# The down projection of a decoder layer in seven half-size products: another order of its streams, a fourth raw buffer, and additions moved to DMA

## The chip, the core and the metric

One core of a Trainium2 chip runs the whole layer as one program. Its engines are TensorE (PE, the matrix multiplications), VectorE (DVE), ScalarE (ACT), GpSimd (POOL) and SyncE (SP). Each works through its own instructions in a fixed order and waits on semaphores for the others. Transfers between HBM and on-chip memory are issued here from SP and from POOL, and 16 DMA engines carry them out. The metric is the device time of one execution in microseconds (us). Lower is better.

## The reference

One layer for 512 tokens of width 2048 in f32. The last part of it, the feed-forward block, is what the change is about:

```python
D_MODEL = 2048; SEQ = 512; D_FF = 5632; CONV_W = 3
...
def conv_ffn(h, w_up, w_conv, b_conv, w_down):
    u = h @ w_up                                  # (512, 2048) @ (2048, 11264)
    up = jnp.pad(u, ((0, 0), (CONV_W - 1, 0), (0, 0)))
    conv = b_conv
    for j in range(CONV_W):
        conv = conv + w_conv[j] * up[:, j:j + S]
    gate, val = jnp.split(conv, 2, axis=-1)
    return (jax.nn.silu(gate) * val) @ w_down     # (512, 5632) @ (5632, 2048)
...
        h = rms_norm(x, g_ffn[l]) * (1.0 + sc_f) + sh_f
        x = x + gt_f * conv_ffn(h, w_up[l], w_conv[l], b_conv[l], w_down[l])
```

Ahead of it stand the modulation by `c @ w_ada`, one combined input projection, two attention branches and an output projection. The change leaves these as they are.

## The kernel before

Every product is done in three matrix multiplications: an operand is split into a high part `hi` (rounded to fp32r by ACT, line 127) and a rest `lo` (subtracted by DVE, line 128), and `mm3` (lines 130 to 133) adds hi·hi, hi·lo and lo·hi in a PSUM bank. In the up and the down projection the kernel saves one product in eight: it cuts both operands into 2 by 2 blocks and forms the four result blocks out of seven products of sums and differences of blocks (`r11`, `r21`, `r22`, `t1` to `t4` for the activations). Sums of the weights are formed on the chip, by DVE, from blocks that are loaded raw.

On-chip memory is handed out by hand. There are 76 slots of 128 x 512 f32 (`get`, `put`, a queue that hands out the slot that was freed longest ago), one area `wraw` for raw weights and one area `wsp` for their hi and lo parts. Whoever takes a slot waits for the slot's last users.

**The up projection** (`seven`, line 926) runs pairs of output blocks, seven steps of 24 matrix multiplications with 256 columns each. At the end of a pair `ffn_out` does the convolution and the gating, and `f_out` (line 1341) writes the result and its sums to HBM (`set_d`), seven kinds of 11 tiles each.

**The down projection** (lines 1425 to 1663) reads them back. It is a loop over 110 steps: five phases (`phases`, line 1573) of NK = 22 steps. A phase keeps 4 or 6 accumulators in PSUM banks, and a step adds one block of 128 rows of `w_down` to all of them:

- C for `fp` = 0 and 1 (half of the output columns each): three products (r11, t1, t4), 6 accumulators, 18 matrix multiplications of 128 x 512 a step. `fetch_c` loads 768 KB of weights a step, `form_c` (line 1449) adds two blocks.
- S for `fp` = 0 and 1: three products (t2, t3, r22), 18 matrix multiplications a step. `fetch_s` loads 768 KB into the raw buffer and 256 KB into a slot `x`; `form_s` (lines 1460 to 1463) does three additions and gives `x` back.
- D: the product r21 for both halves, 4 accumulators, 12 matrix multiplications a step, 512 KB of weights and no sums.

The order is C0, C1, S0, S1, D. Step q is made ready like this: `fetch(q + 3)` issues its loads from SP into one of three raw buffers `dr` (512 x 3 columns of `wraw`), `form(q + 2)` does the sums and the split into one of three pairs `dh`, `dl`. The activations are loaded by `load_set` (line 1431) through POOL into a slot and split: r11, t1, t4 four steps ahead in C0; t2, t3, r22 in C1, each when an old pair is dropped (`sets_after`); r21 in D. The first loads of the down projection are written behind the end of `seven`.

At the end of a phase the last two steps are done accumulator by accumulator, and each accumulator is evicted as it is finished (lines 1654 to 1657). In C, `ev_c` adds the products, multiplies by the gate row, adds the residual `x1` (loaded by POOL, line 1485, multiplied in line 1486, added in line 1487) and writes four partial results per token block to HBM (`q1l`, `q1r`, `q2l`, `q2r`, line 1488). In S and D, `ev_s` and `ev_d` load a partial result (`part`, line 1519), multiply the new product by the gate row, add (`leave`, line 1523) and write `out` from SP (line 1524). `gate_row` (lines 786, 787) makes a gate row of two transfers by POOL: a plain load, and a load of a row of `b_ada` that is broadcast and added to the tile by the DMA itself (`accum_op`).

The program is written in this order, but the instruction order on each engine is set by a planner that runs a timeline of its own over the program when it is built: an instruction can be placed behind later ones of the source if the plan does not have its inputs yet. On the chip the order on each engine is then fixed.

Of the kernel before, what the change touches and what calls it, by code (L numbers as in the profile page):

```python
# [18 lines left out]
P = 128  # L19
# [12 lines left out]
def trunk_layer_kernel(  # L32
# [5 lines left out]
    n_slots=76,  # L38
# [22 lines left out]
    cur = [None] * n_slots  # L61
    free = deque(range(n_slots))
    held = {}

    def get(dt=F32):
        i = free.popleft()
        if cur[i] is None or cur[i].dtype != dt:
# [13 lines left out]
    def put(*ts):  # L81
        for t in ts:
            i = held.pop(id(t))
            if isinstance(i, int):
                free.append(i)
            else:
                rfree.append(t)
# [5 lines left out]
    wraw = pool.tile([P, NR * WB], F32, name="wraw")  # L93
# [4 lines left out]
    rfree.extend(wsp[:, o:o + T] for o in range(2 * NH * WB, 2 * NP * DW - T + 1, T))  # L98
    cnt = {"wt": 0, "half": 0, "at": 0}
# [826 lines left out]
    def seven(src, n_pairs, rs, pairs_of_banks, fin, tick=None, near_end=None):  # L926
# [109 lines left out]
        for q in range(len(steps) + AHEAD):  # L1036
# [18 lines left out]
            if near_end and q - AHEAD == len(steps) - 7:  # L1055
                near_end()
# [27 lines left out]
    def reload_mq():  # L1084
        for t in h[:KH]:
            put(*t)
        mqT.extend(reload(mq_d))
# [330 lines left out]


    seven(w_ups, len(UP_PAIRS), operands(h2, tsum), [(bank[2 * i], bank[2 * i + 1]) for i in range(4)], ffn_out)  # L1420
    for t in h2 + [x for ts in tsum for x in ts]:
        put(*t)


    rfree.clear()
    dr = [wraw[:, i * DW:(i + 1) * DW] for i in range(3)]
    dh = [wsp[:, i * DW:(i + 1) * DW] for i in range(NP)]
    dl = [wsp[:, (NP + i) * DW:(NP + i + 1) * DW] for i in range(NP)]
# [29 lines left out]
    def form_s(t, x):  # L1458
        a, d, b = t[:, 0:512], t[:, 512:1024], t[:, 1024:1536]
        V.tensor_tensor(a, a, x, ALU.subtract)  # L1460
        put(x)
# [3 lines left out]
    def fetch_d(_, k, t):  # L1465
# [4 lines left out]
              for n in ("q1l", "q1r", "q2l", "q2r") for fp in range(2) for tt in range(2)}  # L1470

    def gate_of(db):
        t = get()
# [3 lines left out]
    keep = {}  # L1477

    def ev_c(fp):
        g = {}  # L1480

        def base(n, t, tt, src):
            f, r = int(n[1]) - 1, n[2] == "r"
            xt = get()
            G.dma_start(xt, x1_d[fp * 2 + f][2 * r + tt])
            V.tensor_tensor(t, src, g[f], ALU.mult)
            V.tensor_tensor(t, t, xt, ALU.add)
            G.dma_start(part_d[n, fp, tt], t)
            put(xt)

        def ev(i, tt, b):
            t = get()
            if i == 0:
                if tt == 0:
                    g.update({0: gate_of(fp * 2), 1: gate_of(fp * 2 + 1)})
                p = get()
                A.activation(p, b, AF.Copy)
                keep[fp, tt] = p
                base("q1l", t, tt, p)
                put(t)  # L1500
                return
            p = keep[fp, tt]
            V.tensor_tensor(t, b, p, ALU.add)
            if i == 1:
                q = get()
                base("q2r", q, tt, t)
                put(q)
                base("q1r", t, tt, t)
            else:
                base("q2l", t, tt, t)  # L1510
                put(keep.pop((fp, tt)))
                if tt == 1:
                    put(*g.values())
            put(t)
        return ev

    def part(n, fp, tt):
        t = get()
        G.dma_start(t, part_d[n, fp, tt])
        return t  # L1520

# [191 lines left out]
```

## Time and profile before

| | us |
|---|---|
| median of 3 runs | 2752.41 (2751.76 to 2757.78) |
| the profiled execution | 2749.67 |
| its span, first to last instruction | 2747.9 |
| PE busy in the span | 2614.8 (95%) |
| DVE busy | 2171.5 (79%) |
| ACT busy | 1203.0 (44%) |
| POOL busy | 316.4 (12%) |

The profiled execution is 1.8 us longer than its span and 2.7 us shorter than the median. Busy shares are means over stages with different limits; matrix multiplications are pipelined, so that two of them overlap in the records, and the rate is better read from how many of them a stretch holds. The views used below are: the busy time of each engine in chosen stretches (with the number of instructions, the granted share of TensorE's clock, the busy share of the DMA engines and the rate in GB/s), the waits (engine and line, what it waited for, us in total, times, longest), the chain of work that ended last (start, us, what), and the groups of instructions (count, busy us, mean ns of one, idle time before).

### The profile page before, as it was taken

The numbers are of one execution on the slowest core, as the hardware profiler recorded it, in microseconds if no ns is written. First come the engines' busy times: TensorE is split into PE (matmuls) and PEld (weight loads), VectorE is DVE, ScalarE is ACT, GpSimd is POOL, SyncE is SP. The second block draws the span as 40 slices with busy tenths as digits, with TensorE's granted clock in tenths as the row PEclk, the third lists the DMA queues.
The fourth block names the chain that finished last, engine by engine and source line by source line (L and its number), as shares of the span: only waits on it lengthen the run. The fifth ranks groups of instructions, "written<-read, shape, count | busy, mean of one in ns | idle before, by whom it ended". The sixth has DMA issues, their size and how long they took to land. (4 is left out here: it accounts for less than half of the span.)

```text
span 2747.9 us, 40904 instructions
## 1 busy us (share of the span) xinstructions
PE 2614.8 (95%) x15352; PEld 2261.5 (82%) x15352; DVE 2171.5 (79%) x3378; ACT 1203.0 (44%) x1726; POOL 316.4 (12%) x602
## 2 busy tenths in 40 slices
PE   6999999999999999999999999999999979968798
PEld 5887787779987767788789999999999968746576
DVE  7977967698877658872878989899999976877775
ACT  4333434334444464222645555555555553522233
POOL 1001011110032222110000000000000120210110
PEclk8999899999999999999999999999999989989999
DMA  9943137655575578963233343434334476976875
GB/s 351 350 132 97 34 109 222 212 187 192 196 230 163 182 255 292 325 222 116 90 113 132 112 142 122 141 125 134 126 121 134 143 268 203 328 261 204 267 253 172
DMA packets 233099, 512.28 MB, mean 186 GB/s; under 512 B 24858, under 2 KB 66228, under 8 KB 232900
## 3 DMA queue, kind: packets, MB, share of 16 engines
q1 hardware_dynamic: 191508, 394.74, 44.1%
q0 software_dynamic: 41360, 114.92, 12.3%
q8 instruction: 120, 1.97, 0.3%
q14 instruction: 79, 0.65, 0.1%
q10 hardware_dynamic: 32, 0.01, 0.0%
HBM read 452.69 MB, written 56.89 MB: 185 GB/s over the span
## 5 line engine op out<-in xcount | busy, mean ns | idle before, releaser
L127 ACT ACTIVATE wsp<-wraw 128x1024 fp32r<-128x1024 f32 (+1 forms) x446 | 509.9, 1146 | 721.2 <-PE bank L1050 329.2
L1050 PE MATMUL bank<-slot,wsp 128*128 128x256 f32 x2592 | 730.4, 282 | 0.4 <-DVE slot L128 0.4
L1049 PE MATMUL bank<-slot,wsp 128*128 128x256 f32 x2544 | 714.5, 281 | 6.8 <-ACT slot L127 3.5
L1051 PE MATMUL bank<-slot,wsp 128*128 128x256 f32 x2544 | 715.3, 281 | 3.3 <-DVE wsp L128 3.3
L128 DVE TENSOR_TENSOR wsp<-wraw,wsp 128x1024 fp32r<-128x1024 f32 (+1 forms) x446 | 591.3, 1327 | 124.1 <-ACT wsp L127 123.4
L133 PE MATMUL bank<-wsp,slot 128*128 128x512 f32 (+2 forms) x1300 | 509.4, 394 | 12.0 <-DVE slot L128 12.0
L132 PE MATMUL bank<-wsp,slot 128*128 128x512 f32 (+2 forms) x1258 | 498.2, 396 | 19.8 <-DVE wsp L128 19.3
L1050 PEld LDWEIGHTS bank<-slot,wsp 128*128 128x128 f32 x2592 | 488.4, 188 | 0.7 <-DVE slot L128 0.6
L131 PE MATMUL bank<-wsp,slot 128*128 128x512 f32 (+2 forms) x1258 | 445.6, 398 | 45.6 <-ACT wsp L127 35.6
L1049 PEld LDWEIGHTS bank<-slot,wsp 128*128 128x128 f32 x2544 | 480.9, 189 | 8.8 <-ACT slot L127 4.0
L1051 PEld LDWEIGHTS bank<-slot,wsp 128*128 128x128 f32 x2544 | 479.8, 189 | 3.8 <-DVE wsp L128 3.7
L119 ACT ACTIVATE wsp<-wraw 128x1024 fp32r<-128x1024 f32 (+4 forms) x182 | 187.2, 1031 | 359.2 <-PE bank L133 199.9
L120 DVE TENSOR_TENSOR wsp<-wraw,wsp 128x1024 fp32r<-128x1024 f32 (+4 forms) x182 | 215.8, 1187 | 161.7 <-ACT wsp L119 161.4
L131 PEld LDWEIGHTS bank<-wsp,slot 128*128 128x128 f32 x1258 | 239.9, 191 | 104.0 <-ACT wsp L127 39.1
L132 PEld LDWEIGHTS bank<-wsp,slot 128*128 128x128 f32 x1258 | 239.5, 190 | 82.5 <-DVE wsp L128 29.7
L133 PEld LDWEIGHTS bank<-wsp,slot 128*128 128x128 f32 x1300 | 246.8, 190 | 67.3 <-DVE slot L128 13.3
L942 DVE TENSOR_TENSOR wraw<-wraw 128x1024 f32<-128x1024 f32 x192 | 234.0, 1219 | 1.5
L132 PE MATMUL bank<-slot,wsp 128*128 128x512 f32 (+1 forms) x574 | 230.6, 402 | 0.0
L133 PE MATMUL bank<-slot,wsp 128*128 128x512 f32 (+1 forms) x533 | 210.8, 404 | 6.1 <-DVE wsp L120 6.1
L131 PE MATMUL bank<-slot,wsp 128*128 128x512 f32 (+1 forms) x533 | 212.5, 405 | 0.0
L736 DVE SCALAR_TENSOR_TENSOR slot<-slot,c_act,slot 128x512 f32<-128x512 f32 x203 | 149.8, 748 | 40.2 <-DMA slot<-in_w_ada 38.5
L127 ACT ACTIVATE slot<-slot 128x512 fp32r<-128x512 f32 x136 | 82.3, 624 | 108.3 <-DMA slot<-t 23.8
(344 smaller groups left out, 3309.2 us busy)
## 6 DMA issues: line engine op xcount, KB each, us to landing
slot<-in_w_ada SPq DMA_DIRECT2D x344, 256.0 KB, 5.4
wraw<-in_w_ups SPq DMA_DIRECT2D x160, 512.0 KB, 4.5
wraw<-in_w_down SPq DMA_DIRECT2D x110, 512.0 KB, 5.1
wraw<-in_w_in SPq DMA_DIRECT2D x50, 512.0 KB, 3.6
wraw<-in_w_down SPq DMA_DIRECT2D x88, 256.0 KB, 5.3
wraw<-in_w_gs SPq DMA_DIRECT2D x32, 512.0 KB, 4.1
wraw<-in_w_o SPq DMA_DIRECT2D x32, 512.0 KB, 5.0
t<-slot POOLq DMA_DIRECT2D x44, 256.0 KB, 5.3
```

The costliest lines, as they stand in the source:

```text
L119: A.activation(hi, raw[:, :w], AF.Copy)
L120: V.tensor_tensor(lo, raw[:, :w], r32(hi), ALU.subtract)
L127: A.activation(dst_hi, src, AF.Copy)
L128: V.tensor_tensor(dst_lo, src, r32(dst_hi), ALU.subtract)
L131: PE.matmul(o, lh, rh, start=first, stop=False)
L132: PE.matmul(o, lh, rl, start=False, stop=False)
L133: PE.matmul(o, ll, rh, start=False, stop=last)
L736: V.scalar_tensor_tensor(acc, ts[i], c_act[:, k:k + 1], acc, op0=ALU.mult, op1=ALU.add)
L942: V.tensor_tensor(o[:, :WN], a[:, :WN], b[:, :WN], op)
L1049: PE.matmul(o, wh[:, ks], rh, start=first and k == 0, stop=False, skip_group_check=True)
L1050: PE.matmul(o, wh[:, ks], rl, start=False, stop=False, skip_group_check=True)
L1051: PE.matmul(o, wl[:, ks], rh, start=False, stop=last, skip_group_check=True)
```

## The change

In the down projection: D comes third (C0, C1, D, S0, S1). There are four raw buffers and a prefetch distance of four steps. The step's raw `x` and the raw activations come from a ring of three slots of their own, evictions from a second ring (`spare`, five slots), and raw activations are loaded by SP. The eviction of C only copies or adds and writes the products `s1`, `s3`, `s4` to HBM; eight jobs a phase, one after each of the following steps, load a product back, multiply it by the gate row, add `x1` by an accumulating DMA and write the partial result. For S0 and D, the partial result is likewise added by an accumulating DMA, and the result is then written to `out`; S1, now the last phase, loads its partial results eight steps ahead and adds them with DVE and POOL. In the last seven steps of the up projection (`near_down`) the first two sets of activations are loaded and split, step 0 is loaded into slots and split, and the loads of steps 1 to 3 are issued. The slots become 74, with one more inside `wraw` that is retired before the down projection.

```diff
-    n_slots=76,
+    n_slots=74,
...
-    wraw = pool.tile([P, NR * WB], F32, name="wraw")
+    wraw = pool.tile([P, 4 * DW], F32, name="wraw")
...
+    cur[n_slots] = wraw[:, NR * WB:NR * WB + T]
+    free.append(n_slots)
...
-            if near_end and q - AHEAD == len(steps) - 7:
-                near_end()
+            if near_end and q - AHEAD >= len(steps) - 7:
+                near_end(q - AHEAD - len(steps) + 7)
...
-    dr = [wraw[:, i * DW:(i + 1) * DW] for i in range(3)]
+    dr = [wraw[:, i * DW:(i + 1) * DW] for i in (1, 2, 3, 0)]
...
+    def rget():
+        return ring.popleft() if ring else get()
...
+    def eget():
+        return spare.popleft()
...
     def load_set(n, i):
-        raw, hi, lo = get(), getr(), getr()
-        G.dma_start(raw, set_d[n][i])
+        raw = rget()
+        SP.dma_start(raw, set_d[n][i])
+        hi, lo = getr(), getr()
         split(hi, lo, raw)
-        put(raw)
+        rput(raw)
...
     def fetch_s(fp, k, t):
+        SP.dma_start(t[:, 512:1536], rows_of(1, k, fp * 1024, 1024))
         SP.dma_start(t[:, 0:512], rows_of(0, k, fp * 1024 + 512, 512))
-        SP.dma_start(t[:, 512:1536], rows_of(1, k, fp * 1024, 1024))
-        x = get()
+        x = rget()
...
+    def store(n, fp, tt, t):
+        G.dma_start(part_d[n, fp, tt], t)
+        spare.append(t)
...
     def ev_c(fp):
...
         def ev(i, tt, b):
+            t = eget()
             if i == 0:
+                ps[tt] = t
+                A.activation(t, b, AF.Copy)
+                G.dma_start(part_d["s1", fp, tt], t)
                 return
+            V.tensor_tensor(t, b, ps[tt], ALU.add)
+            if i == 2:
+                spare.append(ps.pop(tt))
+            store(("s3", "s4")[i - 1], fp, tt, t)
+            if i == 2 and tt == 1:
+                jobs()
+
+        def base(n, src, tt, f, t):
+            V.tensor_tensor(t, t, g[f], ALU.mult)
+            G.dma_start(t, x1_d[fp * 2 + f][2 * (n[2] == "r") + tt], accum_op=ALU.add)
+            store(n, fp, tt, t)
+
+        def jobs():
+            work = [("q2l", "s4", 0, 1), ("q2r", "s3", 0, 1), ("q2l", "s4", 1, 1), ("q2r", "s3", 1, 1),
+                    ("q1l", "s1", 0, 0), ("q1r", "s3", 0, 0), ("q1l", "s1", 1, 0), ("q1r", "s3", 1, 0)]
...
+            def load(u):
+                if u == 0 or u == 4:
+                    g[1 - u // 4] = gate_of(fp * 2 + 1 - u // 4)
+                ts[u] = eget()
+                G.dma_start(ts[u], part_d[work[u][1], fp, work[u][2]])
...
+            later.extend((None, lambda: load(0)))
+            for u in range(8):
+                later.append((lambda u: lambda: (load(u + 1) if u < 7 and u != 3 else None, go(u),
+                                                 load(4) if u == 3 else None))(u))
...
-    def leave(t, q, db, tb):
-        V.tensor_tensor(q, q, t, ALU.add)
-        SP.dma_start(out[tb * P:(tb + 1) * P, db * 512:(db + 1) * 512], q)
-        put(q)
+    def result(t, n, fp, tt, back):
+        db, tb = fp * 2 + int(n[1]) - 1, 2 * (n[2] == "r") + tt
+        G.dma_start(t, part_d[n, fp, tt], accum_op=ALU.add)
+        SP.dma_start(out[tb * P:(tb + 1) * P, db * 512:(db + 1) * 512], t)
+        back(t)
...
+    def ev_f(fp):
...
+            eng.tensor_tensor(q, q, t, ALU.add)
+            SP.dma_start(out[tb * P:(tb + 1) * P, db * 512:(db + 1) * 512], q)
...
+            if i == 1:
+                V.tensor_tensor(t, t, fin[1], ALU.mult)
+                go("q2r", tt, t, V)
+                go("q2l", tt, t, G)
...
     phases = [(fetch_c, form_c, DW, 0, C_, ev_c(0)), (fetch_c, form_c, DW, 1, C_, ev_c(1)),
-              (fetch_s, form_s, DW, 0, S_, ev_s(0)), (fetch_s, form_s, DW, 1, S_, ev_s(1)),
-              (fetch_d, None, 1024, 0, D_, ev_d(0))]
+              (fetch_d, None, 1024, 0, D_, ev_d(0)),
+              (fetch_s, form_s, DW, 0, S_, ev_s(0)), (fetch_s, form_s, DW, 1, S_, ev_f(1))]
...
         if p == 1:
-            for n in ("r11", "t1", "t4"):
+            for n, m in (("r11", "r21"), ("t1", "t2"), ("t4", "t3")):
                 drop_set(n, i)
-            for n in ("t2", "t3", "r22"):
-                load_set(n, i)
+                load_set(m, i)
+        elif p == 2:
+            drop_set("r21", i)
+            load_set("r22", i)
...
+    def near_down(i):
+        if i == 0:
...
+            for n in ("r11", "t1", "t4"):
+                load_set(n, 0)
+            first_form(first_fetch())
...
+        elif i == 2:
...
+            for n in ("r11", "t1", "t4"):
+                load_set(n, 1)
+        elif i == 4:
...
+            for q in (1, 2, 3):
+                fetch(q)
...
-            fetch(q + 3)
+            fetch(q + 4)
...
+            if q == 0:
+                put(*step0)
+                ring.extend(get() for _ in range(3))
+                spare.extend(get() for _ in range(n_slots - 3 - 3 * NK))
...
+        if later and k < NK - 2:
+            f = later.popleft()
+            if f:
+                f()
```

More of the change, by code (lines that the diff above doesn't have):

```diff
@@ L1469, in trunk_layer_kernel @@
     part_d = {(n, fp, tt): dram.tile([P, T], F32, name=f"{n}_{fp}_{tt}")
-              for n in ("q1l", "q1r", "q2l", "q2r") for fp in range(2) for tt in range(2)}
+              for n in ("q1l", "q1r", "q2l", "q2r", "s1", "s3", "s4") for fp in range(2) for tt in range(2)}
+    later = deque()
     def gate_of(db):
-        t = get()
+        t = eget()
         gate_row(t, 20 + db)
         return t
-    keep = {}
+    def store(n, fp, tt, t):
+        G.dma_start(part_d[n, fp, tt], t)
+        spare.append(t)
@@ L1479, in ev_c @@
     def ev_c(fp):
[L1480 to L1489, printed above, removed]
+        ps, g = {}, {}
         def ev(i, tt, b):
-            t = get()
+            t = eget()
             if i == 0:
[L1494 to L1500, printed above, removed]
-                return
[L1502 to L1506, printed above, removed]
-                put(q)
[L1508 to L1514, printed above, removed]
@@ new lines, in gates, with two_right, one_right @@
+        def gates():
+            for f in range(2):
+                g[f] = get()
+                gate_row(g[f], 20 + fp * 2 + f)
+        def two_right(tt):
+            m, n = us[tt], get()
+            V.tensor_tensor(m, m, g[1], ALU.mult)
+            A.activation(n, m, AF.Copy)
+            result(m, "q2r", fp, tt, spare.append)
+            result(n, "q2l", fp, tt, put)
+        def one_right(tt):
+            V.tensor_tensor(ps[tt], ps[tt], g[0], ALU.mult)
+            result(ps[tt], "q1r", fp, tt, spare.append)
@@ new lines, in jobs, with fin_load @@
+        def jobs():
+            later.extend((None, None, gates, None))
+            for tt in range(2):
+                later.append(lambda tt=tt: two_right(tt))
+                later.append(lambda tt=tt: one_right(tt))
+            later.append(lambda: put(*g.values()))
+        return ev
+    fin = {}
+    def fin_load(fp):
+        for f in range(2):
+            fin[f] = get()
+            gate_row(fin[f], 20 + fp * 2 + f)
+        for tt in range(2):
+            for n in ("q2r", "q2l", "q1r"):
+                fin[n, tt] = get()
+                G.dma_start(fin[n, tt], part_d[n, fp, tt])
@@ L1562, in ev_d, with gate, go @@
     def ev_d(_):
+        ts, g = {}, {}
         def ev(fp, tt, b):
-            t = get()
-            V.tensor_tensor(t, b, base[fp], ALU.mult)
-            leave(t, base[fp, tt], fp * 2, tt)
-            put(t)
+            ts[fp, tt] = eget()
+            A.activation(ts[fp, tt], b, AF.Copy)
+            if (fp, tt) == (1, 1):
+                jobs()
+        def gate(fp):
+            g[fp] = gate_of(fp * 2)
+        def go(fp, tt):
+            t = ts[fp, tt]
+            V.tensor_tensor(t, t, g[fp], ALU.mult)
+            result(t, "q1l", fp, tt, spare.append)
+            if tt == 1:
+                spare.append(g.pop(fp))
@@ L1568, in ev_d, with jobs @@
+        def jobs():
+            for fp in range(2):
+                later.extend((lambda fp=fp: gate(fp), None))
+                later.append(lambda fp=fp: go(fp, 0))
+                later.append(lambda fp=fp: go(fp, 1))
         return ev
```

168 lines of the change are left out of this document (97 added, 71 removed).

## The prediction

> **What bounds the kernel now.** First the page's header and slices, to see which engine carries the time.
>
> ```profile
> span 2747.9 us, 40904 instructions
> PE   6999999999999999999999999999999979968798
> ```
>
> PE is full nearly everywhere; the holes are in the last eight slices, the down projection. So I next ask for the busy time by stage, cut where the phases change (columns: stretch, its length, busy us of PE with the number of matrix multiplications, PEld, DVE, ACT, POOL, granted clock, DMA share, GB/s).
>
> ```profile
> 2110.00:2210.00 100.00, 100.00 (x845) 99.80 (x843) 91.49 (x112) 57.13 (x81) 16.66 (x31) 1.00 0.48 160
> 2211.00:2326.00 115.00, 98.90 (x393) 78.06 (x394) 75.78 (x81) 47.26 (x49) 13.69 (x24) 0.93 0.67 227
> 2327.00:2421.00 94.00, 91.85 (x394) 73.80 (x393) 79.22 (x92) 49.03 (x53) 26.99 (x49) 1.00 0.92 316
> 2421.00:2556.00 135.00, 100.28 (x399) 77.06 (x398) 96.28 (x112) 36.47 (x30) 13.72 (x24) 0.89 0.70 222
> 2556.00:2677.00 121.00, 99.19 (x400) 75.75 (x399) 92.65 (x109) 39.66 (x36) 18.67 (x32) 0.94 0.79 265
> 2677.00:2740.00 63.00, 61.92 (x264) 48.98 (x262) 33.74 (x36) 21.23 (x21) 0.00 (x0) 1.00 0.56 180
> ```
>
> The first row is the end of the up projection, the others are C0, C1, S0, S1, D. D runs without a hole: 61.92 us for 264, or 0.2345 us each. At that rate the stages would take 92.2, 92.4, 93.6, 93.8 and 61.9 us. They lose 22.8 (C0), 1.6 (C1), 41.4 (S0), 27.2 (S1) and 1.1 us (D), 94 in all. This is the whole stock that the change can win, since it leaves every matrix multiplication in place.
>
> Next, what PE waited for: around the start, around C1 to S0, inside S0, and around S0 to S1.
>
> ```profile
> PE bank L133 <- DVE slot L128: 12.0, 3, 6.3
> ...
> PE bank L131 <- ACT wsp L127: 17.6, 1, 17.6
> PE bank L131 <- DVE slot L1503: 7.9, 1, 7.9
> ...
> PE bank L132 <- DVE wsp L128: 8.9, 7, 4.6
> ...
> PE bank L131 <- ACT wsp L127: 15.1, 2, 8.3
> ```
>
> The reader is to see that PE never waits for a transfer itself. At the start it waits for the split of the activations (a slot); at the phase changes for the split of the first weights (`wsp`) and, at C1 to S0, for an eviction that frees a bank (line 1503); inside S0 for the rest of the weights. Behind those the chain of work shows the reason (start, us, what), first inside S0, then at S0 to S1:
>
> ```profile
> 2497.81 1.68 DVE wsp L128
> 2499.51 3.91 DMA wraw<-in_w_down
> 2503.43 0.69 DVE wraw L1460
> ...
> 2508.82 7.84 DMA wraw<-in_w_down
> ...
> 2567.90 6.24 DMA out<-slot
> 2574.21 6.35 DMA slot<-in_w_down
> 2580.57 6.81 DMA slot<-in_w_down
> ```
>
> Inside S0 a load starts when a split has freed its raw buffer, and the next sums wait for it: three buffers do not cover a landing. At S0 to S1 the slot for `x` waits for an `out` store, then one `x` load waits for the one before: the slots are short, not the DMA.
>
> **The change part by part.**
>
> *Start in C0.* Sets 0 and 1, step 0 and the loads of steps 1 to 3 move ahead of the last up matrix multiplication. Groups of the down projection (count | busy us, mean ns | idle before):
>
> ```profile
> L128 DVE TENSOR_TENSOR wsp<-wraw,wsp 128x1536 fp32r<-128x1536 f32 x88 | 154.1, 1754 | 24.0 <-ACT wsp L127 23.7
> L128 DVE TENSOR_TENSOR slot<-slot,slot 128x512 fp32r<-128x512 f32 x66 | 43.7, 686 | 3.5 <-ACT slot L127 3.3
> L1460 DVE TENSOR_TENSOR wraw<-wraw,slot 128x512 f32<-128x512 f32 x44 | 30.4, 690 | 38.1 <-DMA wraw<-in_w_down 25.3 <-issue 6.8 <-DMA slot<-in_w_down 5.9
> L1486 DVE TENSOR_TENSOR slot<-slot,slot 128x512 f32<-128x512 f32 x16 | 10.9, 687 | 1.6 <-DMA slot<-in_b_ada 0.8 <-ACT slot L1497 0.7
> L1487 DVE TENSOR_TENSOR slot<-slot,slot 128x512 f32<-128x512 f32 x16 | 10.8, 685 | 0.4 <-DMA slot<-x 0.4
> L1523 DVE TENSOR_TENSOR slot<-slot,slot 128x512 f32<-128x512 f32 x16 | 10.4, 686 | 1.4 <-DMA slot<-q2l 0.7 <-DMA slot<-q1r 0.6
> L127 ACT ACTIVATE wsp<-wraw 128x1536 fp32r<-128x1536 f32 x88 | 130.3, 1489 | 230.6 <-DVE wraw L1463 129.7 <-PE bank L133 43.7 <-DVE wraw L1449 27.0
> ```
>
> The moved DVE work is ten instructions of 0.69 us (six sets, three splits, one sum), 6.9 us. In the up projection's end DVE is busy 91.49 of 100 us, so over 20 us it has 1.7 us free: the rest displaces splits of the old order, which stood there too. PE then has step 0, 18 x 0.2345 = 4.2 us, while the convolution's end (about six DVE instructions, some 4 us) and the sums and splits of steps 1 and 2 (2.4 us each) want DVE, 8.8 us against 8.4 for two steps. I leave 5 of the 22.8 us; bounds 1 and 16 (only the 6.9 us of moved work gained).
>
> *Phase ends.* In C, an eviction drops from 2 x 6 multiplications and additions with their `x1` loads to four additions and two copies; the multiplications follow one a step. The 16 `x1` additions (10.8 us), and 10 of the 16 in line 1523 (6.5 us), leave DVE, two more go to POOL. The slot waits at C1 to S0 and S0 to S1 go with the rings: `x` no longer queues behind a store. What is late next is DVE: at S0 to S1 two steps of sums and splits (2 x 3.8 us) plus four additions (2.7 us) make 10.3 us in 8.4, so 2 us are lost, and twice that with an imperfect order. I leave 1 us at C0 to C1, 3 at D to S0, 4 at S0 to S1; bounds 0 to 2, 1 to 12, 1 to 17 (the present waits).
>
> *Fourth raw buffer.* It gives each load one more step, 4.2 us, more than the 3.9 us that the chain shows as a wait; of the one wait of 7.84 us it covers 4.2. DVE in S does 3 x 0.69 + 1.75 = 3.8 us a step of 4.2, and holds. I leave 2 us in S0 (bounds 1, 10) and 4 in S1, where eight late loads of partial results and gates arrive in one burst (bounds 1, 9).
>
> *More DMA.* New are 12 stores of products and 16 loads back, 256 KB each, 7.3 MB; accumulating `x1` loads replace plain ones. C1 then moves weights 16.2, sets 8.7, stores 1.6, two gate rows 1.0 and jobs 24 x 0.262 = 6.3, together 33.8 MB; D moves 25.4 MB. What the DMA can move beside this load pattern:
>
> ```profile
> 2345.00:2400.00 55.00, 55.00 (x237) 44.35 (x237) 48.15 (x57) 32.08 (x37) 16.13 (x30) 1.00 0.96 329
> 40.00:60.00 20.00, 17.42 (x76) 14.73 (x76) 15.61 (x25) 5.56 (x9) 0.00 (x0) 0.76 1.08 373
> ```
>
> 329 GB/s at a share of 0.96 is 343 at full share: 98.5 us for C1 and 74 for D, 18 us more than PE's 154.8. That is the upper bound; the lower is 0, since jobs can lag into S0, which has room for 5.7 MB. C1 of before ran at 316 GB/s and lost 1.6 us, the nearest row, so I take 10. By the Trainium skill (*DMA: Bandwidth & Descriptors*, Specifications) a core's HBM limit is about 358 GB/s; by that figure, as an estimate, C1 and D would be 11 us over. The trace does not keep to it: it reads 373 in a stretch of large loads.
>
> *Waits added.* Each job is a chain on POOL, in order: load, accumulate, store.
>
> ```profile
> slot<-x POOLq DMA_DIRECT2D x16, 256.0 KB, 5.0
> slot<-gtr POOLq DMA_DIRECT2D x14, 256.0 KB, 5.6
> slot<-in_b_ada POOLq DMA_DIRECT2D x14, 256.0 KB, 6.8
> L787 POOL DMA_DIRECT2D slot<-in_b_ada x14 | 12.8, 915 | 30.1 <-DMA slot<-gtr 26.8 <-DMA wraw<-in_w_down 2.6 <-issue 0.5
> L1485 POOL DMA_DIRECT2D slot<-x x16 | 8.6, 540 | 23.2 <-DVE slot L128 9.6 <-DMA q2r<-slot 7.6 <-DMA q1l<-slot 4.7
> ```
>
> Behind the store that waits for an accumulation (6.8 us, the only accumulating row) stand the next load (0.54) and the next accumulation: 7.9 us a job if nothing is interleaved, and 5.6 + 6.8 us for a gate row. Eight jobs and two gate rows are 88 us at most. They fit in C1, not in D's 62. On SP, an `out` store waits for its accumulation with the weight loads queued behind it, up to 6.8 us; the fourth buffer covers 4.2. These waits are why I left 3 and 4 us in D to S0 and S0 to S1.
>
> *Slots, 76 to 75, and the rest of the kernel.* The row of slot loads in the stages ahead:
>
> ```profile
> L736 DVE SCALAR_TENSOR_TENSOR slot<-slot,c_act,slot 128x512 f32<-128x512 f32 x203 | 149.8, 748 | 40.2 <-DMA slot<-in_w_ada 38.5
> ```
>
> One slot in 76 of 38.5 us is 0.5 us; I take 0, bounds -3 and +3, as the whole order is planned anew.
>
> *The end.* An accumulator of D cost two DVE instructions and a store, one of S1 costs three. PE finishes the last four 1.4 us apart (six matrix multiplications each); DVE, starting with the first of them, is done 12 x 0.69 - 4.2 = 4.1 us after PE, where it was 8 x 0.69 - 4.2 = 1.3: +2 us, bounds 0 and +3. The addition on POOL starts some 1.5 us before the last matrix multiplication ends and may take 4 us without cost; no row shows one of this size. The Trainium skill (*GPSIMD Engine Reference*, 4.1 Engine selection) puts a two-input operation at about twice VectorE's time, by estimate 1.4 us, which would be hidden.
>
> *The sum.* Left over are 5 + 1 + 10 + 3 + 2 + 4 + 4 + 2 = 31 us of the 94, so 63 are gained: 2749.67 - 63 = 2686.7 for the profiled execution. The median of before lies 2.7 us above its profiled execution; 2689 is what I predict for the median.
>
> **The rivals.**
>
> *Nearly all stalls go* (15%). D shows that PE can run without a hole while loads land. For it: 4 to 14 us left. Against it: DVE's 10.3 us in 8.4 at S0 to S1. Time 2662 to 2672.
>
> *POOL's chain holds the evictions of D* (20%). The five spare slots go round; the second eviction of D takes the slot of C1's sixth job, whose store has landed after 12.4 + 4 x 7.9 + 12.4 + 2 x 7.9 + 5 = 77 us of D, and S0's sixth accumulator, 3.5 us after D's 62, needs the evicted bank: 12 us lost, and with the DMA bound taken in full (18 for 10) 20. Against it: POOL's order can interleave two accumulations. Time 2709, with part of the DVE waits of the next rival up to 2730.
>
> *DVE is dragged by the job chain, and the kernel is slower* (6%). If each multiplication stood in DVE's order at its step of the source, DVE would wait for the loads that POOL issues late: 88 us of chain against 42 (ten steps of C1) and 28 (ten of D), 106 us, less 14 of two steps made ready: 92 against 63 gained from the rest, 2781. It decides from 4 us a job, 63 over 16 jobs. Against it: the idle before lines 1486, 1487 and 1523, 48 instructions of just this kind, is 2.5 us in all for DMA, because the plan places them later.
>
> *The change does not do what it says* (4%): the new prefetch still waits for the splits and other slots, and the gain is lost to the DMA bound. 2750.
>
> **How the numbers follow.** My own case has 55%, 2672 to 2708: 31 us left, give or take some 17 by the bounds above, of which not all fall together. With the first two rivals that is 90% on the faster side, where "the same" means within 0.2% or 5.5 us, about what a measurement of this kernel can tell from no change; same 3%, slower 7%. For the range I take 2664 to 2728, leaving out the last two rivals and the tails of the others.
>
> **What the changed profile would show.** The stages, read as above, should be C0 near 98 us, C1 98, D 67, S0 99, S1 100. Right at the start: no wait of PE for a slot's split over 3 us. Right for the rings: no `x` load behind an `out` store in the chain. Right for the fourth buffer: the waits of line 1460 for DMA fall from 25.3 us to under 8. DMA share in C1 over 0.95, if the added traffic is felt. My forecast is wrong if DVE's multiplications wait for loads by tens of us, if POOL's stores end after D, or if the stages before 2210 us come out more than 3 us longer.

## The result, and the profile after

The changed kernel takes 2703.01 us (median of 4 runs, 2700.7 to 2704.46) against 2752.09 us of the kernel before beside it: a ratio of 0.9818, 95% interval 0.9801 to 0.9835. It is 49 us faster, where 63 were forecast. The profiled execution took 2701.86 us, its span is 2699.9 us, 48.0 us less than before.

The stages of the changed kernel, in the view of busy time by stretch (columns as in the prediction), cut at the phase changes: the up projection's end, then C0, C1, D, S0, S1.

```profile
2110.00:2207.00 97.00, 96.26 (x794) 95.05 (x793) 85.99 (x108) 51.58 (x72) 6.45 (x12) 1.00 0.53 176
2207.00:2305.00 98.00, 91.28 (x380) 71.76 (x380) 73.96 (x80) 48.33 (x53) 4.83 (x9) 0.97 0.76 251
2305.00:2398.00 93.00, 93.00 (x400) 74.98 (x399) 70.40 (x75) 47.05 (x49) 21.98 (x34) 1.00 0.98 332
2398.00:2473.00 75.00, 63.71 (x264) 48.55 (x262) 44.14 (x53) 32.77 (x40) 20.11 (x31) 0.97 1.04 340
2473.00:2589.00 116.00, 102.68 (x398) 79.76 (x399) 89.69 (x102) 37.77 (x32) 6.02 (x8) 0.90 0.79 245
2589.00:2689.00 100.00, 93.92 (x396) 73.33 (x394) 78.63 (x90) 32.59 (x25) 14.46 (x20) 1.00 0.78 252
```

Read the length against the matrix multiplications in brackets, at the 0.2345 us that one takes when nothing holds it: C1 needs 92.9 us for its 396 and takes 93, while DMA is busy 98% of the time. D needs 61.9 and takes 75; S0 needs 93 and takes 116. The rest of the document counts a stage from the first matrix multiplication of one phase to that of the next (C0 from the up projection's last), and calls "lost" what goes beyond 0.2345 us for each one in it:

| us | before: length, lost | after: length, lost | forecast length |
|---|---|---|---|
| C0 | 117.0, 24.2 | 98.4, 9.7 | 98 |
| C1 | 94.7, 1.9 | 92.3, 0 | 98 |
| D | 63.4, 1.5 | 75.3, 13.4 | 67 |
| S0 | 134.7, 41.8 | 115.6, 22.7 | 99 |
| S1 | 120.6, 27.7 | 99.7, 6.9 | 100 |
| last matrix multiplication to end of span | 7.7 | 11.5 | 9.7 |
| up projection's end (last matrix multiplication) | at 2209.7 | at 2207.1 | at 2209.7 |

In C0, 18 of the 396 matrix multiplications of the phase stand inside the up projection's end. The lengths add up to 530.4 before and 481.3 after, 49.1 less; the end is 3.8 us longer, and the stages ahead are 2.6 us shorter.

What is missing lies in one place, the end of D and the entry of S0. The waits in these two stages (waiting engine and line, for what, us in total, times, longest), first of PE:

```profile
PE bank L138 <- ACT wsp L134: 16.2, 4, 9.7
PE bank L139 <- DVE wsp L135: 8.2, 6, 4.1
```

and DVE:

```profile
...
DVE slot L135 <- ACT slot L134: 13.5, 6, 6.6
DVE wraw L1476 <- DMA wraw<-in_w_down: 12.6, 12, 2.4
DVE slot L1637 <- DMA slot<-in_b_ada: 6.2, 1, 6.2
```

PE waits 9.7 us at a stretch for split weights, and DVE, which should form them, itself waits 6.6 us for a slot. This one wait ends with the first matrix multiplication of S0, so the table counts it in D: D's own matrix multiplications end at 2463.4 and lose less than 4 of the 13.4 us. The timeline around it (start, us, engine, line, what; in brackets the wait ahead of it) shows whose slot:

```profile
2456.87 0.53 SPq L1448 DMA_DIRECT2D slot<-r  x1
...
2457.49 0.40 SPq L1471 DMA_DIRECT2D slot<-in_w_down  x1
...
2461.95 0.33 SPq L1471 DMA_DIRECT2D slot<-in_w_down  x1
...
2467.82 0.69 DVE L135 TENSOR_TENSOR slot<-slot,slot 128x512 fp32r<-128x512 f32 x1 [6.59 <-ACT slot L134]
2468.54 0.33 SPq L1448 DMA_DIRECT2D slot<-r  x1
2469.22 0.69 DVE L1476 TENSOR_TENSOR wraw<-wraw,slot 128x512 f32<-128x512 f32 x1 [0.71 <-DMA slot<-in_w_down]
2469.94 0.33 SPq L1471 DMA_DIRECT2D slot<-in_w_down  x1
...
2473.07 2.08 PE L138 MATMUL bank<-wsp,slot 128*128 128x512 f32 x4 [9.66 <-ACT wsp L134]
```

Line 1448 loads a raw tile of r22, line 1471 an `x` of S0's first steps; both take their slot from the ring of three. The tile loaded at 2456.87 is split at 2467.82; only then, 0.03 us behind that split, does the next tile of r22 start, and the next `x` only when the sum of line 1476 has given one back. The sum itself then waits 0.71 us more for its `x`, the first of S0, which was issued only at 2457.49, 6 us before D's last matrix multiplication. So the split of r22 and this late `x` end the wait almost together. The DMA issues of these two stages (count, size, median us to landing) say why a slot is held so long: at a DMA share of 1.04 a tile of this kind, nearly all of them r22's, lands in 10.1 us.

```profile
slot<-r SPq DMA_DIRECT2D x13, 256.0 KB, 10.1
slot<-s POOLq DMA_DIRECT2D x8, 256.0 KB, 6.1
slot<-x POOLq DMA_DIRECT2D x8, 256.0 KB, 8.5
```

A long stop can cost more than its own length. Behind this one the granted clock (the last column but two) is at half for 6 us:

```profile
2473.00:2479.00 6.00, 5.62 (x13) 3.70 (x13) 5.56 (x7) 2.23 (x4) 1.08 (x2) 0.50 0.95 320
```

Most of these 13 matrix multiplications start 0.43 us apart instead of 0.2345. By the records of the clock 40 of S0's 396 ran like this, and 7.5 of its 22.7 us are theirs; in the kernel before, 72 in C0, S0 and S1 cost 12.9 us.

The start came as planned: PE waits 4.2 us for the weights of step 1 and 0.6 us for a slot's split, where it lost 12.0 in three waits before.

```profile
PE bank L138 <- ACT wsp L134: 4.2, 1, 4.2
PE bank L138 <- ACT slot L134: 0.6, 1, 0.6
```

### The profile page after: what moved, and what is told of

Its sections match the earlier page's. It is cut to its first block, busy times and chain, and to the rows that moved or that the text cites. A ratio compares the mean times of both kernels' runs of the same rounds, so it can differ in the third digit from the quotient of the medians.

```text
span 2699.9 us, 40940 instructions
## 1 busy us (share of the span) xinstructions
PE 2603.6 (96%) x15352; PEld 2253.9 (83%) x15352; DVE 2154.0 (80%) x3352; ACT 1207.8 (45%) x1736; POOL 303.2 (11%) x555
## 4 chain that ended last, share of the span: by engine, by line
PE 62%; issue 17%; DMA 12%; DVE 6%; ACT 2%; POOL 2%; SPq 0%; DVEq 0%; POOLq 0%; ACTq 0%
PE bank L1057 10%; PE bank L1056 10%; PE bank L1058 10%; PE bank L138 9%; PE bank L139 9%; PE bank L140 9%; DMA wraw<-in_w_down 5%; DVE wsp L135 2%; DMA slot<-t 2%; DMA slot<-in_w_down 1%; DMA slot<-in_w_ada 1%; PE bank L1193 1%; ACT wsp L134 1%; DVE slot L135 1%; DMA slot<-r 1%
## 5 line engine op out<-in xcount | busy, mean ns | idle before, releaser
L139 PE MATMUL bank<-wsp,slot 128*128 128x512 f32 (+2 forms) x1252 | 497.6, 397 | 15.9 <-DVE wsp L135 15.7
```

What stands on the lines that cost most here:

```text
L139: PE.matmul(o, lh, rl, start=False, stop=False)
```

## The experiments

Each time is a median beside runs of the kernel before, with the ratio to it and its 95% interval. "Ring" is the slots for `x` and raw activations, 3 in the changed kernel.

**C1's jobs left out.** C1's eight load, multiply, accumulate, store jobs run in D; this kernel leaves them out, and later phases read the partial results of C0 in their place.

```diff
-            if i == 2 and tt == 1:
+            if i == 2 and tt == 1 and fp == 0:
                 jobs()
```

> The changed kernel, with the eight jobs of C1 left out (no loads of s1/s3/s4, no gate row, no x1 addition, no store; the later phases read the partial results of the other half instead, so their traffic stays). In the changed kernel D and the entry of S0 stand still for 36 us (D 13.4, S0 22.7 over the PE rate). Theory A, the DMA engines are full through D because of the jobs (346 GB/s at a share of 1.03 in D) and S0's first weights land late: S0's entry becomes clean, 20 to 28 us faster than the changed kernel, about 2677, no wait of PE over 4 us between 2460 and 2500. Rival B, the ring of three that r22's raw tiles share with x holds SP: the entry stays, 0 to 6 us faster. Rival C, DVE stands behind D's own gate row: only the last of the four waits (4.5 us) is left.

Measured: 2687.65 us (two runs), 0.9757 (0.9722 to 0.9791), 15 us less than the changed kernel: more than B's 0 to 6, less than A's 20 to 28. D loses nothing (before this edit 13.4 us), S0 still 18.4. The stages D and S0:

```profile
2399.00:2461.00 62.00, 62.00 (x266) 49.71 (x265) 41.46 (x49) 32.83 (x41) 2.52 (x4) 1.00 0.93 309
2461.00:2572.00 111.00, 99.65 (x396) 77.48 (x395) 86.20 (x98) 36.11 (x30) 4.93 (x6) 0.94 0.77 244
```

Without the jobs the tiles of r land in 6.3 us instead of 10.1:

```profile
slot<-r SPq DMA_DIRECT2D x13, 256.0 KB, 6.3
```

So the jobs are needed for D's loss, but they explain only 4 of the 22.7 us in S0.

**Both gate rows of a C phase ahead of its jobs.** They are otherwise loaded one before each half.

```diff
-                if u == 0 or u == 4:
-                    g[1 - u // 4] = gate_of(fp * 2 + 1 - u // 4)
+                if u == 0:
+                    g[1] = gate_of(fp * 2 + 1)
+                    g[0] = gate_of(fp * 2)
```

> The changed kernel, with both gate rows of a C phase loaded ahead of the first job instead of the second one in the middle. In the changed kernel the last four jobs of C1 wait for the second gate row and all four accumulations are issued within 2 us at 2458, when S0's first weights are in flight. Theory A (full DMA at S0's entry): the jobs spread over D, fewer transfers at the entry, 5 to 15 us faster than the changed kernel, 2688 to 2698. Rival B (ring): no change, 2703 +- 3. Rival D, total bytes in C1 and D decide and not their place: no change either, the wait of 10 us is only split otherwise.

Measured: 2697.16 us, 0.9792 (0.9768 to 0.9817); its interval and that of the changed kernel overlap. The median lies in theory A's range, but the profiled execution, the slowest of four, does not show what A forecast there: D still loses 13.3 us, S0 20.1 instead of 22.7. In this profile the second gate row is not quite 3 us of the loss there, and S1 loses 1.9 us more; whether the 6 us between the medians are a gain is open.

**r22's loads left out** (eleven loads of 256 KB; the splits stay).

```diff
-        SP.dma_start(raw, set_d[n][i])
+        if n != "r22":
+            SP.dma_start(raw, set_d[n][i])
```

> The changed kernel, with the eleven loads of r22 left out (the slots are split with what they held). Rival B (ring and SP held by r22's raw tiles, DVE waiting 6.6 us for the split of one): S0's entry becomes clean, 20 us or more faster than the changed kernel. Theory A: 2.9 of 25 MB less in D, a gain in proportion, 3 to 10 us.

Measured: 2679.71 us, 0.9728 (0.9683 to 0.9773), from two runs 14 us apart; the profile is that of the slower one, 2686.72 us. D loses 3.6 and S0 10.4 us, 22 less than in the changed kernel, although the jobs run and DMA is as full as ever in D:

```profile
2404.00:2469.00 65.00, 61.59 (x263) 48.91 (x261) 45.62 (x56) 32.39 (x41) 17.98 (x27) 1.00 1.01 333
2469.00:2572.00 103.00, 95.95 (x395) 74.53 (x396) 84.15 (x96) 35.67 (x30) 8.06 (x11) 0.98 0.86 278
```

A full DMA (share 1.01, 333 GB/s) is thus not by itself the loss. Left out here are both 2.9 MB and the time that r22 holds ring slots; the runs further down part these two.

**The kernel before with the new slots alone** (74, and one more in the raw area).

```diff
-    n_slots=76,
+    n_slots=74,
...
+    cur[n_slots] = wraw[:, NR * WB:NR * WB + T]
+    free.append(n_slots)
```

> The kernel before, with the slots of the changed kernel alone: 74 slots and one in wraw, wraw as large as in the changed kernel, three raw buffers used. In the changed kernel the stages ahead of the up projection ended 6.6 us earlier than in the kernel before (7.0 us later at 440 us, 14 us made up between 850 and 1140 us). If the slots' order is the reason, this kernel shows the same shift: 2741 to 2748, up projection starting near 1405. If the whole plan differs for another reason (the source behind it), it shows none: 2750 to 2756.

Measured: 2756.76 us, 1.0012 (0.9995 to 1.0028). The stages ahead end 6.8 us earlier (up projection's last matrix multiplication at 2202.9 instead of 2209.7), as the first theory had it, but no time is gained: the old down projection is 17.8 us longer. C0 loses 5.9 us less and D 1.9 less, C1 loses 3.6, S0 8.5 and S1 13.5 more. Why, no run shows. The 2.6 us that the changed kernel gains upstream fit this: 6.8 us from the other order of the slots, less 4.2 us for the 18 matrix multiplications of step 0 that now stand there.

**Three raw buffers.**

```diff
-    dr = [wraw[:, i * DW:(i + 1) * DW] for i in (1, 2, 3, 0)]
+    dr = [wraw[:, i * DW:(i + 1) * DW] for i in (1, 2, 0)]
...
-            fetch(q + 4)
+            fetch(q + 3)
```

> The changed kernel with three raw buffers and a prefetch distance of three steps, the rest of the change kept (S0 115.6 and S1 99.7 us in the changed kernel, 2703 us in all). If the fourth buffer carries the gain of S1, as the prediction has it (four of the 24 us left over), S1 goes back to 110 to 118 us, S0 loses 5 to 10 us more, C0 and C1 stay within 3 us: 2720 to 2735. Rival: the long waits of S0 and S1 went with the rings (x no longer stands behind an out store) and the fourth buffer is spare: S0 and S1 within 3 us, 2700 to 2708.

The prefetch distance goes from four to three with it. Measured: 2714.61 us, 0.9867 (0.9849 to 0.9886), 12 us more than with four and between the two ranges. S1 loses 17.1 us instead of 6.9, as forecast. But C1 loses 7.7 and D 21.8 (8 more each), and S0 only 12.7, 10 less. The stages C1 and D:

```profile
2302.00:2402.00 100.00, 95.44 (x396) 74.22 (x394) 70.86 (x76) 46.51 (x50) 19.64 (x30) 0.98 0.93 308
2402.00:2486.00 84.00, 70.12 (x267) 51.76 (x265) 45.50 (x54) 33.18 (x41) 23.41 (x36) 0.94 0.98 317
```

The fourth buffer is what lets C1 run at 332 GB/s without a hole; here it moves 308 and loses 8 us. D and S0 together lose 34.5 us, against 36.1, so that most of it stands earlier, not more of it; why, no run shows.

**The first steps prepared behind the up projection**, as before the change.

```diff
-          near_end=near_down)
+          )
+    for i in range(5):
+        near_down(i)
```

> The changed kernel with the preparation of the first steps (sets 0 and 1, step 0, loads of steps 1 to 3) written behind the last step of the up projection, as before the change. If the early preparation is what took C0 from 117 to 98.4 us, C0 loses 12 to 15 us more than now, all later stages stay within 2 us, and the time is 2713 to 2718. Rival: the preparation only moves work that delays the up projection's last steps; then that projection ends 4 us earlier, C0 loses 8 us more, and the time is 2705 to 2709.

Measured: 2721.53 us, 0.9888 (0.9866 to 0.991): the early preparation is worth 18.5 us, more than either theory gave. C0 loses 33.0 us, 28.4 of them in one wait of PE:

```profile
PE bank L138 <- ACT slot L134: 28.4, 1, 28.4
```

The up projection ends 3.6 us earlier, about the rival's 4, but not for the rival's reason: the 18 matrix multiplications of step 0, 4.2 us, no longer stand in it. So the moved loads and splits cost nothing there that shows. Written late, the new start is worse than the old one (24.2): step 0's slots are then loaded by SP at 2224 to 2228 us, behind loads of the later steps.

**The phases in the old order**, with the rest of the change (C0, C1, S0, S1, D).

```diff
-              (fetch_d, None, 1024, 0, D_, ev_d(0)),
-              (fetch_s, form_s, DW, 0, S_, ev_s(0)), (fetch_s, form_s, DW, 1, S_, ev_f(1))]
+              (fetch_s, form_s, DW, 0, S_, ev_s(0)), (fetch_s, form_s, DW, 1, S_, ev_s(1)),
+              (fetch_d, None, 1024, 0, D_, ev_l)]
...
-            for n, m in (("r11", "r21"), ("t1", "t2"), ("t4", "t3")):
+            for n, m in (("r11", "t2"), ("t1", "t3"), ("t4", "r22")):
```

> The changed kernel with the phases in the old order C0, C1, S0, S1, D (t2, t3 and r22 loaded in C1, r21 in S1; the partial results of D loaded eight steps before the end and added by DVE). Theory: the 36 us lost at the end of D and the entry of S0 come from r22's loads, which share three slots with x, and from C1's jobs, both pressed into the short phase D. With the old order these fall into C1 and S0: C1 loses up to 5, S0's entry under 10, D nothing: 2675 to 2688. Rival: S0's first steps start late because four raw buffers, x and the evictions' DVE work meet there, whatever phase is ahead: S0 loses 20 to 25 us, D nothing, and the time is 2690 to 2702.

Measured: 2723.01 us, 0.9894 (0.9873 to 0.9914), 20 us slower than with D third. Both expectations missed. C1 loses 12.2, S0 29.5, S1 22.4, D 2.6. The timeline of SP and DVE at the entry of S0, where PE waits 19.3 us (from 2416.5 to 2435.8):

```profile
2410.52 0.33 SPq L1471 DMA_DIRECT2D slot<-in_w_down  x1
...
2415.20 0.33 SPq L1448 DMA_DIRECT2D slot<-t  x1
2416.42 0.33 SPq L1448 DMA_DIRECT2D slot<-r  x1
...
2424.97 0.33 SPq L1448 DMA_DIRECT2D slot<-r  x1
2426.73 12.57 SPq L1471 DMA_DIRECT2D slot<-in_w_down  x4
...
2431.32 0.69 DVE L135 TENSOR_TENSOR slot<-slot,slot 128x512 fp32r<-128x512 f32 x1 [4.63 <-ACT slot L134]
2432.05 0.69 DVE L1476 TENSOR_TENSOR wraw<-wraw,slot 128x512 f32<-128x512 f32 x1
```

After the `x` of 2410.52 no other is issued until 2426.73: the last activations (line 1448) hold the ring, each until its split. The sum that PE waits for stands in DVE's order right behind the split, at 2431.32, of the tile that could be loaded only at 2424.97. Three tiles in two steps share the three slots with `x` in this order, one tile in two steps when D stands between. S1, where r21 is now loaded beside `x`, loses 22.4 us instead of 6.9.

**r22's last four tiles loaded in S0** (steps 3 to 9) instead of D's last eight steps.

```diff
             drop_set("r21", i)
-            load_set("r22", i)
+            if i < 7:
+                load_set("r22", i)
+        elif p == 3 and 1 <= i < 5:
+            load_set("r22", i + 6)
```

> The changed kernel with the last four of the eleven r22 tiles loaded and split in the steps 3, 5, 7 and 9 of S0 instead of the last eight steps of D; the same loads and splits in all. Theory of the ring: r22 and x share three slots and SP's order at D's end, so D and S0 together lose 15 to 22 us less (36 now): 2682 to 2689. Rival, traffic: four loads are 1 MB, 3 us at 340 GB/s, and D's end is late because C1's jobs and the gate rows take the DMA: 2698 to 2701. Rival, VectorE: the multiplication that waits for D's gate row holds S0's sums; nothing changes: 2700 to 2706.

Measured: 2692.96 us, 0.9785 (0.9763 to 0.9808). With the same loads in all, D loses 3.7 us instead of 13.4, S0 18.6 instead of 22.7. The time is 10 us less, between the theory's 14 to 21 and the traffic rival's 2 to 5; in the profile (2687.26 us, the fastest of four) D and S0 lose 13.8 us less, just under the theory's 15 to 22. S0 does not pay for D's gain: it loses 4.1 us less, although the four tiles are now loaded in it beside `x`.

**A ring of four slots.**

```diff
-    n_slots=74,
+    n_slots=75,
...
-                ring.extend(get() for _ in range(3))
-                spare.extend(get() for _ in range(n_slots - 3 - 3 * NK))
+                ring.extend(get() for _ in range(4))
+                spare.extend(get() for _ in range(n_slots - 4 - 3 * NK))
```

> The changed kernel with 75 slots instead of 74, the additional one in the ring of x and raw activations, which then has four slots. Theory: at D's end and in S0 a load of x waits in SP's order for a slot that r22's tile holds until its split; with four slots D and S0 together lose 10 to 18 us less (36 now), the rest stays: 2686 to 2694. Rival: not the slots but the landings under a full DMA (8 to 10 us for r22 and x) make them late; D and S0 lose at most 4 us less, and the time is 2698 to 2705. The one slot more in the stages ahead gives within 3 us either way.

Measured: 2683.02 us, 0.9743 (0.9717 to 0.9769), 20 us faster than the changed kernel, outside its interval. The profiled execution, the slowest of four, is 15.9 us faster than the changed kernel's, and D and S0 together lose 15.8 us less, within the theory's 10 to 18. The stages C0, D, S0:

```profile
2209.00:2304.00 95.00, 91.47 (x386) 72.31 (x385) 72.87 (x79) 47.66 (x52) 4.83 (x9) 0.98 0.78 263
...
2397.00:2460.00 63.00, 62.13 (x264) 49.14 (x264) 39.24 (x46) 29.69 (x35) 13.48 (x22) 1.00 1.04 360
2460.00:2572.00 112.00, 100.28 (x398) 77.65 (x399) 90.45 (x105) 37.11 (x30) 12.15 (x16) 0.94 0.87 267
```

One slot takes D's loss from 13.4 to 1.3 us with every job and every tile still in it, at 360 GB/s instead of 340. S0 loses 19.0 instead of 22.7. C0 loses 5.5 instead of 9.7, although the ring does not exist before step 0; that is probably the other order of the slots, and the up projection ends 2.0 us later. SP now issues the first `x` of S0 26 us earlier than in the changed kernel (2457.49 there):

```profile
2431.62 0.34 SPq L1471 DMA_DIRECT2D slot<-in_w_down  x1
```

This run, with the one without C1's jobs, settles D: with the jobs the landings are long, and a ring of three is short of slots for such landings; the rate itself is no limit. In S0 PE now waits in small pieces, and one of them is the wait that the second rival of the prediction had named, D's eviction (line 1628) behind the store of a job, with 3.5 us where that rival had 12:

```profile
PE bank L139 <- DVE wsp L135: 5.9, 5, 2.6
PE bank L138 <- ACT slot L1628: 3.5, 1, 3.5
PE bank L138 <- ACT wsp L134: 3.1, 3, 2.1
```

**Ring of four, four tiles in S0 (steps 5 to 11), gate rows first, S1's last additions on DVE.**

```diff
-                go("q2l", tt, t, G)
+                go("q2l", tt, t, V)
```

> Four things together on the changed kernel: the ring of four slots (75 in all), the last four tiles of r22 loaded in steps 5, 7, 9 and 11 of S0, both gate rows of a C phase loaded ahead of its first job, and S1's last additions for q2l on VectorE instead of GpSimd. If slots and the burst at D's end are two separate causes, D and S0 lose 12 to 18 us together instead of 36, and the time is 2678 to 2686; if they are one cause told twice, it stays at the 2693 of the kernel with the four tiles moved alone (to 2690). After the last matrix multiplication VectorE has two additions more and POOL none: if POOL's additions double the time of those that run beside them (1.37 instead of 0.68 us, twice), the two cancel, and 11.0 to 11.6 us stay there (11.5 now); if POOL's work was free, it becomes 12.7.

Measured: 2681.03 us, 0.974 (0.9716 to 0.9764), the same as the ring of four alone. D and S0 lose 4.8 and 14.9 us, 19.7 together (20.3 with the ring alone). The time lies in the range for two causes, but only because the ring alone already does; against the ring alone, moving the tiles wins nothing, as it would if slots and burst were one cause told twice. Four edits ran together here, so this is argued, not shown. The end is 11.8 us, above the 11.6 expected if the two cancel and far from the 12.7 if POOL's work was free; with POOL's additions and the same ring it is 12.3.

**Ring of four, gate rows first, each job's store one step later.**

```diff
-            store(n, fp, tt, t)
+            return n, fp, tt, t
...
+                    ts[u] = base(*work[u], ts[u])
+                if u > 0:
+                    store(*ts.pop(u - 1))
```

> The changed kernel with the ring of four slots (75 in all), both gate rows of a C phase loaded ahead of its first job, and the store of each of C's jobs issued one step later, behind the next job's accumulation, so that GpSimd's queue no longer stands still between an accumulation and its store. With the ring alone D lost 1.3 and S0 19.0 us, 2683 us in all. Theory: S0's rest comes from C1's jobs, whose chain runs past D's end, so that D's eviction waits for a spare slot (9.5 us of ScalarE there) and four multiplications stand among S0's first sums; a chain done within D gives back 6 to 10 us: 2673 to 2678. Rival: S0's first three steps are short of VectorE and of landings by themselves, and 2680 to 2685 stays.

Measured: 2687.93 us, 0.9767 (0.974 to 0.9794). The theory fell: S0 loses 21.3 us instead of 19.0, and the time is above the rival's range too, its interval overlapping that of the ring alone. POOL's standing between an accumulation and its store costs nothing that can be won this way.

**Ring of four, C1's jobs left out** (the edits of those two runs together).

> The ring of four slots (75 in all) with C1's eight jobs left out (S1 and S0 read back C0's partial results instead), so neither their transfers nor their multiplications run in D. If jobs and ring are separate causes of the loss at D's end and in S0, S0's 19.0 us (ring alone) fall to 8 to 12, and the time is 2671 to 2677. Rival: the jobs cost only because the ring was short; then S0 stays at 16 to 19, and the time is 2679 to 2684.

Measured: 2677.34 us (two runs), 0.9732 (0.9698 to 0.9766). S0 loses 14.1 us, between the two theories: the jobs cost 5 of its 19.0. Of the rest, one wait of PE is 5.7 us, and 13 matrix multiplications at half the clock behind it cost 2.3. DVE stands 5.4 us at that time at the multiplication by D's gate row, with sums of S0 behind it in its order. The waits of PE, then of DVE:

```profile
PE bank L138 <- ACT wsp L134: 5.7, 1, 5.7
PE bank L139 <- DVE wsp L135: 4.3, 4, 2.2
```

```profile
DVE slot L1637 <- DMA slot<-in_b_ada: 5.4, 1, 5.4
```

## Why the prediction was right, and where it fell short

The sign, the size and the range held: 2689 forecast, 2703 measured, in 2664 to 2728. The sum left 31 us of the stock; by the same count 49 were left. Three parts of the change were taken away one by one, and each carries a share of the gain: the early start is worth 18.5 us, the fourth buffer 12, and D in third place, which has no term of its own in the sum, 20 (with three ring slots; the three need not add up). No run takes away the second ring or the additions moved to DMA, so their share is argued only. Part of the range was luck: the 10 us kept for the DMA rate were needed for it only to 3, and the rest made up for a quarter of what the step from D to S0 had wrong. Term by term:

- **Start in C0: 5 and 1 left, 5.5 measured** (98.4 us against 92.9 for 396 matrix multiplications, with those of step 0 inside the up projection). Right, with its cause: without the early preparation 18.5 us go.
- **More DMA in C1 and D: 10 left, 12.8 measured, and the reason was wrong.** C1 ran at a DMA share of 0.98 and lost nothing; D lost its 13.4 us to the ring, as the ring of four shows, at 360 GB/s with 1.3 us lost. Of the 12.8 us, 9.7 are the wait for S0's first weights, which belongs to the next term; what is left for the rate is 3. The estimate from the row with 343 GB/s at full share is refuted as a limit. The Trainium skill (*DMA: Bandwidth & Descriptors*, Specifications) gives about 358 GB/s as the limit of a core. The trace is at that figure in D, 360 over 63 us, and the 373 over 20 us of the kernel before are above it.
- **D to S0 and inside S0: 3 and 2 left, 22.7 measured, 32.4 with the wait at the entry. This step failed.** "The slot waits at C1 to S0 and S0 to S1 go with the rings" held for `out` stores: none stands ahead of an `x` load for more than 0.6 us. But the ring was counted only against `x`. Three slots serve `x` with two steps in flight and r22 with a landing of 10.1 us at a DMA share of 1.04, where the prediction worked with landings of 5.0 to 6.8 us. The upper bounds, 12 and 10, reach 22 together; what was taken was near their lower end.
- **S0 to S1 and S1: 4 and 4 left, 6.9 measured.** Right; with three raw buffers S1 goes to 17.1. Line 1476's waits for weights (line 1460 before), in the groups of the down projection, fell from 25.3 to 19.7 us only, where under 8 was forecast:

```profile
L1476 DVE TENSOR_TENSOR wraw<-wraw,slot 128x512 f32<-128x512 f32 x44 | 30.3, 690 | 27.8 <-DMA wraw<-in_w_down 19.7 <-DMA slot<-in_w_down 6.8 <-DVE wsp L135 0.8
```

  S1 came out as forecast all the same: for the most part these waits of DVE were not passed on to PE, and they were the wrong sign to name.
- **Waits added.** The multiplications wait for nothing in DVE's order, as argued, with one exception, line 1637, 6.2 us. Where it stood alone, in the last experiment, it became a PE wait of 5.7 us: the rival of DVE dragged by the chain, with one instruction instead of sixteen. One of the prediction's own signs of being wrong did come: C1's jobs end after D. Their last store is issued at 2472.6, 9 us behind D's last matrix multiplication; the prediction had said that the chain does not fit in D's 62 us and had priced this in its second rival only.
- **The end: 2 left, 3.8 measured**, over the bound of 3. The prediction's own working, 4.1 against 1.3 us, gives 2.8 and not the 2 it took; and POOL's additions were costed at nothing, while DVE pays 1.4 us for them (below).
- **The stages ahead: 0, measured -2.6**, in the bounds.

The sum is 5.5 + 12.8 + 22.7 + 6.9 + 3.8 - 2.6 = 49.1, 18 more than 31; the stock counted to the ends of the phases is 97.1 instead of 94, which leaves 15 us between 2686.7 and the 2701.86 of the profiled execution.

Open is what S0 still loses with four ring slots and no jobs, 14.1 us: 5.7 are D's gate row and 2.3 the slow clock behind it; for the rest no run took one cause away. A share may be DVE, busy 90 of 112 us in S0 with the ring alone, with the order that the plan gave it. That S0 loses 10 us less with three raw buffers is not explained either. Each edit also lets the planner order everything anew, so differences of 2 or 3 us in a stage are not traced to the edit.

## What to carry to other kernels

Count a ring against everyone who takes from it, with the landing time under the load that the change itself makes, not under today's: one slot of 256 KB was worth 20 us by the medians and 16 in the profiles, about as much as the whole new order of the phases. A DMA at a share of 1.0 is no loss in itself; look at who holds a buffer while waiting for it. Count a stop of PE with the slow matrix multiplications behind it. When work goes to a second engine at the end, look at whether the first one slows down.

## What the runs showed of the hardware that was not expected

An addition on POOL doubles the time of a DVE addition beside it if that reads two operands from slots, which lie in SBUF; an operand from a PSUM bank does not count. POOL's two additions at the end of the changed kernel:

```profile
2689.01 1.26 POOL L1604 TENSOR_TENSOR slot<-slot,slot 128x512 f32<-128x512 f32 x1 [64.69 <-DVE slot L1615]
2690.89 1.26 POOL L1604 TENSOR_TENSOR slot<-slot,slot 128x512 f32<-128x512 f32 x1 [0.63 <-DVE slot L1615]
```

and DVE at the same time:

```profile
2688.84 0.68 DVE L1613 TENSOR_TENSOR slot<-bank,slot 128x512 f32<-128x512 f32 x1
2689.44 1.37 DVE L1615 TENSOR_TENSOR slot<-slot,slot 128x512 f32<-128x512 f32 x1
2690.74 0.68 DVE L1613 TENSOR_TENSOR slot<-bank,slot 128x512 f32<-128x512 f32 x1
2691.34 1.37 DVE L1604 TENSOR_TENSOR slot<-slot,slot 128x512 f32<-128x512 f32 x1
2692.63 0.68 DVE L1619 TENSOR_TENSOR slot<-slot,slot 128x512 f32<-128x512 f32 x1
```

The two that read a slot and a slot beside POOL take 1.37 us, the two that read a PSUM bank and a slot 0.68 us beside the same POOL instruction; the last line, behind POOL's end, is at 0.68 us with two slots too. In the run with these additions on VectorE, nothing runs on POOL there, and line 1615 (1616 in that run) takes 0.68 us each time:

```profile
2672.16 0.68 DVE L1616 TENSOR_TENSOR slot<-slot,slot 128x512 f32<-128x512 f32 x1
```

This is what the Trainium skill (*SBUF — State Buffer*, Who interferes with whom) states of a DVE instruction with two SBUF inputs and a GpSimd instruction that reads SBUF; the trace agrees, 1.37 against 0.68 us. POOL's 1.26 us also agree with the estimate of 1.4 in the prediction; what they cost DVE, twice 0.69 us, was not in the sum.

Accumulating transfers landed later than plain ones of the same size: 8.5 us for `x1` into a slot against 6.1 us for the products in D and S0 of the changed kernel, both issued by POOL. Four of the eight were issued within 2 us of each other at 2458 and landed after 7.8, 9.6, 11.1 and 12.6 us, so what the accumulation alone costs is not shown.
